# Order of the first conv buffers' state copies, and the place of the group norm among the z projections, in a hybrid pooling / SSD step

## The chip, the cores and the metric

The kernel runs on one core of one Trainium2 chip. The metric is device time in microseconds (us) of one execution; lower is better. A core has a matrix engine (PE, its weight loads shown as PEld), a vector engine (DVE), an activation engine (ACT), a general engine (POOL) and a queue engine (SP). In this kernel SP only issues loads of weights and activations; POOL issues most other transfers.

## The reference

One layer (DEPTH is 1) of a streaming encoder is computed for 384 rows of 2048 features: 256 rows of one new stream and 8 running streams of 16 rows. All data is float32.

```python
u = rmsnorm(x);  proj = u @ w_in          # columns: pool | z | x,B,C | dt | gates
A = pool_mixer(proj[pool])                # causal means of 2, 4, 8, 16 rows minus self, per-group map
xbc = silu(causal_conv(proj[xBC], state_conv))   # depthwise, width 4
y, h = ssd_scan(x, dt, A, B, C, h0)       # 64 heads of 64, state 128, 8 groups
y = y + d_skip * x
hg = y * silu(z)                          # gated norm: within each of the 8 groups of 512 columns
a_ssd = hg * rsqrt(mean(hg * hg) + EPS) * ssd_norm
m = sigmoid(gA) * (A @ w_pool_proj) + sigmoid(gB) * (a_ssd @ w_ssd_proj)
x = x + rmsnorm(m @ w_out)
x = x + rmsnorm(relu(rmsnorm(x) @ w_up) ** 2 @ w_down)
```

The last rows of the pooling and conv inputs and the SSD states are outputs too.

## The kernel before, in words

Every large product is made to float32 accuracy out of three products of a rounded format. A weight tile of 128x1024 is loaded by SP (`wfetch`), ACT copies its high part (`wh`, line 70) and DVE subtracts to get the low part (`wl`, line 71). PE then runs high by high (L101), high weight by low input (L102) and low weight by high input (L103). `wsplit` notes the last pair of such instructions in `cut`. There are three buffers each for the raw, the high and the low tile, and `take` keeps splits two half projections ahead of the one in use.

`proj` multiplies one 128-column block: two halves of 24 matmuls each. In the middle stage the eight SSD groups run one after the other. Group `g` has six projections with a convolution behind them (x, B, x, C, x, x) and four z projections (`zproj(0)` to `zproj(3)`). Among them PE does short products of the scan: those of the previous group's second pair of heads after the fifth conv projection, those of this group's first pair after the fourth z projection. The names that matter here:

- `conv_in`: DVE scales a projection into one of three conv buffers (L599). ACT then copies the three previous rows of each running stream out of the tile `cst_` ("cstate" in the profile) into the buffer (L606), passes the rows between blocks on (L607) and saves the new state (L608). `taps` does the convolution: ACT L616, three DVE L618, ACT L622 with the SiLU.
- `fside`: two DVE products on the decay tile E (L846). `dside`: a DVE product on the state `hs` (L852). `zproj` ends with a DVE scaling of its PSUM result into `zs` (L1039) and a SiLU on ACT (L1040). `final` forms `y` and `z*y` (L885, L896, L897), and squares are summed into `ssum` by ACT (L899, L902) and POOL (L903).
- `finish(prev)` calls `norm_bc` for the previous group: ACT rounds `ssum` (`nh_g`, L197), DVE makes the low part (`nl_g`, L198), PE sums over the partitions by two matmuls with a matrix of ones (`bc_g`: L201 reads `nh_g`, L202 reads `nl_g`), DVE scales the sum (L204), and ten more DVE instructions find the inverse root (L187 to L191). `store(prev)` (L913) scales the four `zs` tiles by it.

Each engine runs its own queue in order. The order of a queue is planned before the run: the planner goes by its own estimate of when each instruction's inputs are there, and among those that it holds to be ready it takes the one that stands first in the program. So instructions of an engine need not stand in the program's order. Two helpers add order: `behind(ins)` puts the instructions of a block that are on the engine of `ins` somewhere behind `ins`; `later()` does so for the last weight split on ACT and on DVE. The matmuls of a half projection are put behind the last matmul of the one before. The two matmuls of `norm_bc` are put behind the matmul that was last when `finish` was called.

Of the kernel before, what the change touches and what calls it, by code (L numbers as in the profile page):

```python
# [33 lines left out]
def build(ctx, tc, io):  # L34
# [21 lines left out]
    def behind(ins):  # L56
        return nullcontext() if ins is None else tc.issue_after(ins.ins)
# [19 lines left out]
    @contextmanager  # L77
    def later():
        with behind(cut[0]), behind(cut[1]):
            yield  # L80
# [10 lines left out]
    def even_odd(a):  # L91
        return a.rearrange("p (n a) -> p a n", a=2)

    def halves(a):
        return a.rearrange("p (a n) -> p a n", a=2)
# [40 lines left out]
    def proj(units, rhs, name, hook=None):  # L136
        o = bank[0](f"pj_{name}")[:, :T]
        for q, src in enumerate(units):
            half(o, q, take(src, f"{name}_{q}"), rhs)
            if hook:  # L140
                hook()
            tick()
        return o
# [50 lines left out]
    def norm_bc(pool, sumsq, n, name, after=None):  # L194
        h = pool.tile([P, T], F32R, tag="nr", name=f"nh_{name}", bufs=2)
        l = pool.tile([P, T], F32R, tag="nr", name=f"nl_{name}", bufs=2)
        s.activation(h, sumsq, AF.Copy)  # L197
        v.tensor_tensor(l, sumsq, h.bitcast(F32), ALU.subtract)  # L198
        o = sstile(f"bc_{name}")[:, :T]
        with behind(after):  # L200
            te.matmul(pairs(o), onesr, woven(h), start=True, stop=False)  # L201
            te.matmul(pairs(o), onesr, woven(l), start=False, stop=True)  # L202
        hm = sumsq
        v.tensor_scalar(halves(hm), even_odd(o), -0.5 / n, -0.5 * EPS, ALU.mult, ALU.add)  # L204
        a = pool.tile([P, T], F32, tag="nr", name=f"na_{name}", bufs=2)
        y = pool.tile([P, T], F32, tag="nr", name=f"ny_{name}", bufs=2)
        return newton(y, a, hm)
# [11 lines left out]
    def in_units(i):  # L219
        return [win[i - 5, 0], win[i - 5, 1]]  # L220
# [358 lines left out]
    with tc.tile_pool(name="phd", bufs=2, reuse_waits="tile") as pd, tc.tile_pool(  # L579
# [10 lines left out]
        ncv = [0]  # L590

        def conv_in(ui, c, hook=None):
            ps = proj(in_units(ui), xg, f"x{c}", hook)
            b = cbuf[ncv[0] % 3]
            ncv[0] += 1
            with later():
                for a in range(2):
                    c12 = slice(a * 12, a * 12 + 12)
                    v.tensor_tensor(  # L599
                        b[:, c12, 3:],  # L600
                        even_odd(ps)[:, a].rearrange("p (b t) -> p b t", b=12),
                        seg(rstd)[:, c12],
                        ALU.mult,
                    )
            with later() if 3 < ncv[0] <= 6 else behind(silu[0]):
                s.copy(b[:, 16:, :3], cst_[:, c, 1:])  # L606
            s.copy(b[:, 1:16, :3], b[:, 0:15, 16:])  # L607
            s.copy(cst_[:, c], b[:, 15:, 16:])  # L608
            return b

        silu = [None]
# [13 lines left out]
        def conv(ui, c, tag, nb, hook=None):  # L625
            return taps(conv_in(ui, c, hook), c, tag, nb)
# [50 lines left out]
        def pload(S):  # L677
            S.hs = pd.tile([P, NB, 2 * P], F32, tag="hs", name=f"hs{S.nm}")
            gp.dma_start(S.hs, io["ssm"][S.qd])
# [163 lines left out]
        def fside(S, h2):  # L843
            Eq = S.E[:, h2 * 2 : h2 * 2 + 2]
            with dve_later():
                v.tensor_tensor(Eq, Eq, S.D.cbm.unsqueeze(1).to_broadcast([P, 2, 512]), ALU.mult)  # L846

        def dside(S):
            hv = S.hs.rearrange("p b (h q) -> p b h q", h=4)
            dv = decb[:, S.h0 : S.h0 + 4, :].rearrange("p h b -> p b h").unsqueeze(3)  # L850
            with dve_later():
                v.tensor_tensor(hv, hv, dv.to_broadcast([P, NB, 4, 64]), ALU.mult)  # L852
# [52 lines left out]
        def finish(D):  # L905
            D.bc = norm_bc(pd, D.ssum, 512, f"g{D.g}", last[0])
# [26 lines left out]
        prev = None  # L933
        for g in range(G + 1):
# [34 lines left out]
            D.p = [pair(D, jp) for jp in range(2)]  # L969
            D.xs, D.zs = [], []  # L970
            b0 = conv_in(u0, g * 4)

            def first():
# [33 lines left out]
            if g:  # L1007
                fside(prev.p[1], 1)
            cside(D)
            b2 = conv_in(u0 + 4, g * 4 + 2)  # L1010
            S = D.p[0]
            S.py = mmtile(f"py{S.nm}")
# [22 lines left out]
            def zproj(j):  # L1035
                ps = proj(in_units(u0 + 6 + j), xg, f"z{g}_{j}")
                z = pd.tile([P, T], F32, tag="zs", name=f"zs{g}_{j}", bufs=8)
                with later():
                    v.tensor_tensor(halves(z), even_odd(ps), halves(rstd), ALU.mult)  # L1039
                    s.activation(z, z, AF.Silu)  # L1040
                D.zs.append(z)
# [7 lines left out]
                bside(D)  # L1049
            dside(S)  # L1050
            zproj(1)
            pload(D.p[1])
            fside(S, 0)
            fside(S, 1)
            zproj(2)
            if g:
                finish(prev)
            zproj(3)
            S1 = D.p[1]
            S1.py = mmtile(f"py{S1.nm}")  # L1060
# [10 lines left out]
            prev = D  # L1071
# [514 lines left out]
```

## Time and profile before

| | |
|---|---|
| time, three runs | 2636.21, 2636.32, 2637.59 us; median 2636.32 |
| profiled execution | 2635.75 us, of which the span of the instructions is 2633.9 |
| PE busy | 2622.0 us |
| PE weight load busy | 2523.3 us |
| DVE busy | 1572.8 us |
| ACT busy | 1160.2 us |
| POOL busy | 368.1 us |
| granted TensorE clock | 0.999 |

The SSD stage runs from about 419 us to 1200 us of the span. A row of the timeline gives the start, the duration, the engine, the line, the operation, the tiles (written<-read), shape, count, and in brackets how long the engine sat idle before it and what ended that. Rows of the same kind that follow each other are merged and counted (x2). The records of neighbours overlap a little. A row of the waits gives the waiting line and the one that released it, the total in us, the number of times, and the longest.

### The profile page before, as it was taken

To read this page: it belongs to the slowest core of one execution; us is meant where nothing else is said; L and a number is where in the kernel's file an instruction comes from. 1 tells how busy PE (TensorE), PEld (TensorE's weight loads), DVE (VectorE), ACT (ScalarE), POOL (GpSimd) and SP (SyncE) were. 2 spreads that over 40 slices of the span, in tenths; PEclk is the share of its full clock that TensorE was granted. 3 is DMA by queue.
4 is the path that set the end of the run, shared out by engine and by line. 5 is a ranking of instruction groups with operands and counts; after the bars stand their busy time and mean duration, and the time that the engine had idled before them with its cause. 6 is when DMAs were issued, how large, how long until landed. Compare 5 with 4: busy or idle time off the path is not lost.

```text
span 2633.9 us, 40787 instructions
## 1 busy us (share of the span) xinstructions
PE 2622.0 (100%) x16189; PEld 2523.3 (96%) x16189; DVE 1572.8 (60%) x2286; ACT 1160.2 (44%) x1789; POOL 368.1 (14%) x545
## 2 busy tenths in 40 slices
PE   9999999999999999999999999999999999999998
PEld 9999999999999999999999989999999999989897
DVE  6685335799999999867444336434444444444446
ACT  6443224657565756555333336433333333333233
POOL 0000002245344444421000000000000000000000
PEclk9999999999999999999999999999999999999999
DMA  7544446667676676657554544444444444444443
GB/s 276 149 134 156 147 148 218 205 207 239 223 239 211 234 230 236 225 190 261 169 160 160 192 149 133 142 137 134 135 135 136 135 136 136 136 136 136 135 135 130
DMA packets 134255, 456.33 MB, mean 173 GB/s; under 512 B 20544, under 2 KB 27520, under 8 KB 129072
## 3 DMA queue, kind: packets, MB, share of 16 engines
q1 hardware_dynamic: 103552, 361.44, 43.0%
q0 software_dynamic: 23456, 77.47, 8.4%
q10 hardware_dynamic: 7056, 14.81, 1.7%
q8 instruction: 127, 2.08, 0.3%
q14 instruction: 64, 0.52, 0.1%
HBM read 409.27 MB, written 44.37 MB: 172 GB/s over the span
## 4 chain that ended last, share of the span: by engine, by line
PE 96%; DMA 1%; DVE 1%; issue 1%; ACT 0%; POOL 0%; SPq 0%; DVEq 0%; POOLq 0%; ACTq 0%
PE pj_up L101 6%; PE pj_up L102 6%; PE pj_up L103 6%; PE wd L156 6%; PE wd L154 6%; PE wd L155 6%; PE pj_x L101 5%; PE pj_x L103 4%; PE pj_x L102 4%; PE pj_sp L103 3%; PE pj_sp L102 3%; PE pj_sp L101 3%; PE pj_z L103 3%; PE pj_z L102 3%; PE pj_z L101 3%; PE pj_gb L101 2%
## 5 line engine op out<-in xcount | busy, mean ns | idle before, releaser
L101 PE MATMUL pj_up<-x1h,wh_up 128*128 128x384 f32 (+1 forms) x1024 | 333.7, 326 | 0.0
L102 PE MATMUL pj_up<-x1l,wh_up 128*128 128x384 f32 (+1 forms) x1024 | 333.4, 326 | 0.0
L103 PE MATMUL pj_up<-x1h,wl_up 128*128 128x384 f32 (+1 forms) x1024 | 333.4, 326 | 0.0
L71 DVE TENSOR_TENSOR wl_wd<-w_wd,wh_wd 128x1024 fp32r<-128x1024 f32 x126 | 154.3, 1225 | 240.5 <-ACT wh_wd L70 240.5
L154 PE MATMUL wd<-wh_wd,hh 128*128 128x512 f32 x756 | 286.5, 379 | 0.0
L155 PE MATMUL wd<-wl_wd,hh 128*128 128x512 f32 x756 | 286.5, 379 | 0.0
L156 PE MATMUL wd<-wh_wd,hl 128*128 128x512 f32 x756 | 286.5, 379 | 0.0
L70 ACT ACTIVATE wh_wd<-w_wd 128x1024 fp32r<-128x1024 f32 x126 | 133.1, 1057 | 321.6 <-PE wd L156 261.2
L70 ACT ACTIVATE wh_up<-w_up 128x1024 fp32r<-128x1024 f32 x126 | 133.1, 1056 | 292.1 <-PE pj_up L102 231.7
L71 DVE TENSOR_TENSOR wl_up<-w_up,wh_up 128x1024 fp32r<-128x1024 f32 x126 | 154.3, 1225 | 178.2 <-ACT wh_up L70 178.0
L101 PE MATMUL pj_x<-xgh,wh_x 128*128 128x384 f32 x768 | 252.0, 328 | 0.0
L103 PE MATMUL pj_x<-xgh,wl_x 128*128 128x384 f32 x768 | 250.5, 326 | 0.7 <-DVE wl_x L71 0.7
L102 PE MATMUL pj_x<-xgl,wh_x 128*128 128x384 f32 x768 | 250.4, 326 | 0.0
L102 PEld LDWEIGHTS pj_up<-x1l,wh_up 128*128 128x128 f32 x1024 | 193.6, 189 | 0.2
L101 PEld LDWEIGHTS pj_up<-x1h,wh_up 128*128 128x128 f32 x1024 | 193.6, 189 | 0.2
L103 PEld LDWEIGHTS pj_up<-x1h,wl_up 128*128 128x128 f32 x1024 | 193.6, 189 | 0.0
L101 PE MATMUL pj_z<-xgh,wh_z 128*128 128x384 f32 x512 | 166.9, 326 | 0.0
L102 PE MATMUL pj_z<-xgl,wh_z 128*128 128x384 f32 x512 | 166.9, 326 | 0.0
L103 PE MATMUL pj_z<-xgh,wl_z 128*128 128x384 f32 x512 | 166.9, 326 | 0.0
L101 PE MATMUL pj_sp<-abh,wh_sp 128*128 128x384 f32 x512 | 166.9, 326 | 0.0
L102 PE MATMUL pj_sp<-abl,wh_sp 128*128 128x384 f32 x512 | 166.9, 326 | 0.0
L103 PE MATMUL pj_sp<-abh,wl_sp 128*128 128x384 f32 x512 | 166.9, 326 | 0.0
(351 smaller groups left out, 6371.5 us busy)
## 6 DMA issues: line engine op xcount, KB each, us to landing
w_up<-w_up SPq DMA_DIRECT2D x128, 512.0 KB, 3.4
w_wd<-w_down SPq DMA_DIRECT2D x128, 512.0 KB, 3.4
w_x<-w_in SPq DMA_DIRECT2D x96, 512.0 KB, 4.0
w_z<-w_in SPq DMA_DIRECT2D x64, 512.0 KB, 4.2
w_sp<-w_ssd SPq DMA_DIRECT2D x64, 512.0 KB, 3.5
w_ga<-w_ga SPq DMA_DIRECT2D x32, 512.0 KB, 3.6
w_pp<-w_pp SPq DMA_DIRECT2D x32, 512.0 KB, 3.5
hs<-ssm POOLq DMA_DIRECT2D x16, 1024.0 KB, 6.5
```

The lines of the kernel that those rows point to most:

```text
L70: cut[0] = s.activation(h, w, AF.Copy)
L71: cut[1] = v.tensor_tensor(l, w, h.bitcast(F32), ALU.subtract)
L101: te.matmul(out, wh, xh, start=first, stop=False, **how)
L102: te.matmul(out, wh, xl, start=False, stop=False, **how)
L103: return te.matmul(out, wl, xh, start=False, stop=last, **how)
L154: te.matmul(out, mh, vh, start=k == 0 and b != held, stop=False, skip_group_check=b == held)
L155: te.matmul(out, mh, vl, start=False, stop=False, skip_group_check=b == held)
L156: last[0] = te.matmul(out, ml, vh, start=False, stop=k == nk - 1, skip_group_check=b == held)
```

## The change

The copies of L606 for the first three conv buffers are put behind the last weight split, as those of buffers four to six already are. Before, the first had no such order, and the second and third were behind the last SiLU of a convolution (`silu[0]`). The call of `finish(prev)` in groups 1 to 7 moves from behind `zproj(2)` to behind `zproj(1)`, ahead of `pload` (a transfer that POOL issues) and of the two `fside` calls.

```diff
@@ -602,7 +602,7 @@
-            with later() if 3 < ncv[0] <= 6 else behind(silu[0]):
+            with later() if ncv[0] <= 6 else behind(silu[0]):
                 s.copy(b[:, 16:, :3], cst_[:, c, 1:])
             s.copy(b[:, 1:16, :3], b[:, 0:15, 16:])
             s.copy(cst_[:, c], b[:, 15:, 16:])
@@ -1049,12 +1049,12 @@
             dside(S)
             zproj(1)
+            if g:
+                finish(prev)
             pload(D.p[1])
             fside(S, 0)
             fside(S, 1)
             zproj(2)
-            if g:
-                finish(prev)
             zproj(3)
```

## The prediction

> **What bounds the kernel now.** I read the page first, then what PE waited for, then the timeline of DVE, PE, ACT and POOL through the z projections and round the start of the SSD stage. The page:
>
> ```profile
> span 2633.9 us, 40787 instructions
> PE 2622.0 (100%) x16189; PEld 2523.3 (96%) x16189; DVE 1572.8 (60%) x2286; ACT 1160.2 (44%) x1789; POOL 368.1 (14%) x545
> PE 96%; DMA 1%; DVE 1%; issue 1%; ACT 0%; POOL 0%; SPq 0%; DVEq 0%; POOLq 0%; ACTq 0%
> ```
>
> PE is busy for 2622.0 of 2633.9 us and makes 96% of the chain that ended last. Whatever the edits do to other engines counts only where PE waits. All that PE waited for (us in total, times, longest):
>
> ```profile
> PE warm_o L242 <- DVE warm L238: 1.2, 1, 1.2
> PE su L861 <- DVE xs L885: 0.9, 1, 0.9
> PE pj_x L103 <- DVE wl_x L71: 0.7, 1, 0.7
> PE pj_p L103 <- DVE wl_e L304: 0.3, 1, 0.3
> PE pj_p L318 <- DVE xgl L280: 0.2, 1, 0.2
> ```
>
> That is 3.3 us, of which the first, fourth and fifth lie far ahead of anything edited. So the change can win at most 0.9 + 0.7 = 1.6 us, or 0.06%. It can lose much more: every new wait of PE is added to the span as it stands, and there are seven groups in which `finish` moves. About 0.2% (5.3 us) is what a measurement of this kernel can tell from no change.
>
> **The norm moved, its instructions.** `finish` has one ACT, two PE and twelve DVE instructions (L198, L204 and ten of the root) and no transfer; their number and sizes stay. DVE in the z phase of group 1, where z1 and z2 stand for the second and third z projection:
>
> ```profile
> 570.50 2.35 DVE L71 TENSOR_TENSOR wl_z<-w_z,wh_z 128x1024 fp32r<-128x1024 f32 x2
> 572.77 2.36 DVE L846 TENSOR_TENSOR E<-E,cbm 128x1024 f32<-128x1024 f32 x2
> 575.04 0.55 DVE L1039 TENSOR_TENSOR zs<-pj_z,rstd 128x384 f32<-128x384 f32 x1
> 575.50 1.22 DVE L71 TENSOR_TENSOR wl_z<-w_z,wh_z 128x1024 fp32r<-128x1024 f32 x1
> 576.64 0.55 DVE L198 TENSOR_TENSOR nl_g<-ssum,nh_g 128x384 fp32r<-128x384 f32 x1
> 577.13 1.23 DVE L71 TENSOR_TENSOR wl_z<-w_z,wh_z 128x1024 fp32r<-128x1024 f32 x1
> 579.82 0.56 DVE L1039 TENSOR_TENSOR zs<-pj_z,rstd 128x384 f32<-128x384 f32 x1 [1.47 <-PE pj_z L103]
> 580.29 0.55 DVE L204 TENSOR_SCALAR ssum<-bc_g 128x384 f32<-128x384 f32 x1
> 580.80 1.22 DVE L71 TENSOR_TENSOR wl_x<-w_x,wh_x 128x1024 fp32r<-128x1024 f32 x1
> 588.08 0.56 DVE L191 SCALAR_TENSOR_TENSOR ny_g<-na_g,ny_g 128x384 f32<-128x384 f32 x1
> ```
>
> The row at 570.50 holds the low parts of both halves of z2, that at 575.04 takes the result of z1. The PE rows are z1's last matmul, the first two of z2, and the norm's first product in groups 1 and 7:
>
> ```profile
> 571.66 0.33 PE L103 MATMUL pj_z<-xgh,wl_z 128*128 128x384 f32 x1
> 571.82 0.33 PE L101 MATMUL pj_z<-xgh,wh_z 128*128 128x384 f32 x1
> 571.98 0.33 PE L102 MATMUL pj_z<-xgl,wh_z 128*128 128x384 f32 x1
> 579.62 0.33 PE L201 MATMUL bc_g<-nh_g,onesr 128*128 128x384 f32 x1
> 1105.59 0.33 PE L201 MATMUL bc_g<-nh_g,onesr 128*128 128x384 f32 x1
> ```
>
> Before, the norm's products came at 579.62, right behind z2, and `nl_g` had been ready since 577.19. That left 2.6 us of slack up to L202 at 579.78. Between group 1 and group 7 lie 1105.59 - 579.62 = 525.97 us, so a group takes 87.66.
>
> After the change the products belong right behind z1: L201 at 571.82, L202 at 571.98. Their other inputs are there:
>
> ```profile
> 554.88 4.00 POOL L903 TENSOR_TENSOR ssum<-ssum,ysq 128x384 f32<-128x384 f32 x1 [0.41 <-ACT ysq L902]
> 567.18 0.51 ACT L197 ACTIVATE nh_g<-ssum 128x384 fp32r<-128x384 f32 x1
> ```
>
> The sum ends at 558.88 and `nh_g` at 567.69, both well ahead. What is not there is `nl_g`. DVE is behind at this point: the low parts of z2 end at 572.85, 0.9 us after z1 has ended (571.99), and z1's result is fetched 3 us late.
>
> **Where `nl_g` will stand.** Ahead of the new `finish` in the program stand the splits of z2 and the scaling of z1; behind it the two E products. `nl_g` was ready from 567.69 on but never ran ahead of the z2 splits, so the planner saw no gap for it there, and the move does not lift it over instructions that still precede it. It does lift it over E. So I put `nl_g` where the first E stands, at 572.77, ending at 573.32.
>
> **Where the two products will stand.** The planner put two E products ahead of the scaling of z1, although that stands earlier in the program. So when it chose the second E, one E product (1.2 us) after the z2 splits, it held z1 to be unfinished still. In its account DVE finishes the z2 splits over 1.2 us before z1 ends; in the trace it does 0.9 us after. The planner is thus out by some 2 us, and an `nl_g` of 0.55 us ends, by its account, some 0.6 us or more before z1 does. The norm's products are then ready when z1 ends, and stand ahead of z2 in the program. They are placed between z1 and z2, and z2's 48 matmuls queue behind L202.
>
> **The sum of the new waits.** In each group L202 has its turn at 571.98 + 87.66 (g - 1), and `nl_g` ends 0.55 us after the start of the first E. The hand-over to PE is taken from the wait of `su` quoted below: L885 ends at 1118.46, PE starts at 1118.51, 0.05 us. The starts of E in groups 2 to 7:
>
> ```profile
> 660.46 2.35 DVE L846 TENSOR_TENSOR E<-E,cbm 128x1024 f32<-128x1024 f32 x2
> 748.30 2.35 DVE L846 TENSOR_TENSOR E<-E,cbm 128x1024 f32<-128x1024 f32 x2
> 836.05 2.35 DVE L846 TENSOR_TENSOR E<-E,cbm 128x1024 f32<-128x1024 f32 x2
> 924.53 2.35 DVE L846 TENSOR_TENSOR E<-E,cbm 128x1024 f32<-128x1024 f32 x2
> 1011.10 2.35 DVE L846 TENSOR_TENSOR E<-E,cbm 128x1024 f32<-128x1024 f32 x2
> 1100.03 2.35 DVE L846 TENSOR_TENSOR E<-E,cbm 128x1024 f32<-128x1024 f32 x2
> ```
>
> E's start + 0.60 less the turn of L202 gives, for groups 1 to 7: 1.39, 1.42, 1.60, 1.69, 2.51, 1.42, 2.69, together 12.7 us. Group 5 is larger because its second split waited for ACT's high part:
>
> ```profile
> 923.39 1.23 DVE L71 TENSOR_TENSOR wl_z<-w_z,wh_z 128x1024 fp32r<-128x1024 f32 x1 [1.03 <-ACT wh_z L70]
> ```
>
> Bounds: if the planner lets three of z2's matmuls (0.16 us apart) in ahead of the products, each wait is 0.5 us shorter, 9.2 us in all. If it takes E first and the products only when `nl_g` is ready by its account, each wait approaches its error of 2 us or a little over, up to 17.5 us in all at 2.5 each. I take 12.7, the one that the rows give.
>
> **What else moves.** L204 and the ten of the root (580.29 to 588.64, with other splits between) come some 6 us earlier, where DVE has other work and 1.47 us idle. PE can lose there only if z3's low parts come late. They were done at 576.72 and 578.36; the first is wanted from 579.94 (z3 begins one matmul, 0.16 us, behind L202 at 579.78), the second 24 matmuls later, at 583.8, and both later still by PE's new wait. The root is a chain in which each step needs the one before, and in the rows above a split that stands later in the program (580.80) was let in behind its first step, L204. So z3's splits will be let in too. I cost this at nothing; the cover is 3.2 us on the first half. A root put wholly ahead of it takes some 6 us of DVE (eleven steps of 0.56), and would cost PE about 2 us a group. `pload` is a POOL issue that `finish` has no instruction in front of. The E products slip by 0.5 us or more and are wanted by the scan's products only behind z3.
>
> **What goes.** In group 7 alone PE waited in the state update:
>
> ```profile
> 1117.85 0.61 DVE L885 SCALAR_TENSOR_TENSOR xs<-xs,vec,Y 128x384 f32<-128x384 f32 x1
> 1118.51 0.71 PE L861 MATMUL su<-xd,Bd 32*128 32x256 f32 x13 [0.94 <-DVE xs L885]
> ```
>
> The root ran ahead of L885 on DVE; in group 1 it ends at 588.64, which in group 7 corresponds to 588.64 + 525.97 = 1114.6, and L885 came at 1117.85. With the root moved to z2's window, eleven DVE instructions that stand ahead of L885 are out of its way by then, and the 0.94 goes. Next late there would be what released the other six groups, in which PE did not wait.
>
> **The copies.** The other wait of 0.7 us is that of the fifth half projection on its low part:
>
> ```profile
> 425.25 0.54 POOL L583 DMA_DIRECT2D cstate<-state_conv  x1 [4.58 <-DMA ma_scr<-sg]
> 422.78 1.06 ACT L70 ACTIVATE wh_x<-w_x 128x1024 fp32r<-128x1024 f32 x1 [2.84 <-PE pj_x L102]
> 433.32 0.22 ACT L606 COPY cbuf<-cstate 128x24 f32<-128x24 f32 x1 [9.48 <-DMA cstate<-state_conv]
> 433.44 1.06 ACT L70 ACTIVATE wh_x<-w_x 128x1024 fp32r<-128x1024 f32 x1
> 438.82 0.62 ACT L622 ACTIVATE xs<-cacc,vec 128x384 f32<-128x384 f32 x1 [1.31 <-DVE cacc L618]
> 439.34 0.20 ACT L606 COPY cbuf<-cstate 128x24 f32<-128x24 f32 x1
> ```
>
> ACT waits for the state's transfer with the next split (433.44) queued behind the copy. When the first `conv_in` reaches its copy, the last split is the fourth of the stage, 422.78; the copy stands behind that already. The new order adds nothing, and the wait stays. The second and third copies are freed from the SiLU before them and can use ACT's idle time (1.31 us ahead of 438.82), 0.2 us each. No PE wait follows there. I cost this edit at 0, between -0.7 (the copy goes behind the fifth split after all) and +0.5 (a freed copy pushes a split, two copies and a gap).
>
> **Sum.** 12.7 - 0.94 + 0 = 11.8 us. The profiled execution, 2635.75, would be 2647.5; it is 0.57 below the median of the runs, so the median becomes 2648.1.
>
> **Rivals.**
> *No wait behind z1.* The planner finds `nl_g` a place ahead of the z2 splits (say at 570.50), or puts the products deep into z2, 1.4 to 2.7 us behind its start. Then PE waits for nothing new, the 0.94 goes, and the time is 2636.3 - 0.9 = 2635.4, with the copies at best 2634.7. It decides once `nl_g` ends before its product's turn, 1.8 us (12.7 / 7) earlier than I place it in the mean group. For it: `nh_g` is ready at 567.69, 2.8 us ahead of the z2 splits. Against it: `nl_g` was just as free to go there before and did not.
> *Long waits.* E, E and the scaling of z1 run ahead of `nl_g`, and the products still stand right behind z1: 2.8 us more in each group (2.36 + 0.47), 12.7 + 7 x 2.8 = 32.3 us, 2636.3 + 32.3 - 0.9 = 2667.7. Against it: the planner does not put E ahead of what stands earlier and is ready.
> [...]
> *The change does nothing to the order that matters*: `nl_g` and the products land where they were, 2636.3.
>
> **How the numbers follow.** The forecast gets 0.63, no wait 0.26, long waits 0.05, nothing 0.06. The forecast's own range is from 2636.3 + 9.2 - 0.9 - 0.7 = 2643.9, to 2636.3 + 17.5 - 0.9 + 0.5 = 2653.4. The range to hold 8 in 10 needs the no-wait rival as well: 2635.0 to 2653.0. Slower by over 0.2% means above 2641.6: the forecast but for 0.02 of it, and the long waits, 0.66. Within 0.2%: no wait, nothing, and that 0.02, less 0.01, is 0.33. Faster by over 0.2% would need more than PE now waits for in all, 0.01.
>
> **What would show it.** Right: among PE's waits `bc_g` L202 for DVE `nl_g`, seven times, 1.4 to 2.7 us; L201 right behind z1 in each group; `nl_g` between the z2 splits and the first E; no wait of `su`; the wait of `pj_x` still about 0.7. Wrong: `bc_g` with no wait, or L201 in the midst of z2, or `nl_g` ahead of the z2 splits; or a new wait of `pj_z` L103 on a split, which would mean that the root stands ahead of it.

## The result, and the profile after

The changed kernel took 2648.84 us in the median of six runs (2646.74 to 2652.73), the kernel before 2636.32 in six (2635.30 to 2637.59): a ratio of 1.005, 95% interval 1.0037 to 1.0063. That is 12.5 us slower, against the forecast 2648.1. In the profiled execution (2647.98 us) the span grew by 12.3 us, from 2633.9 to 2646.2. The head of the page, and all that PE waited for:

```profile
span 2646.2 us, 40773 instructions
PE 2624.9 (99%) x16189; PEld 2525.1 (95%) x16189; DVE 1572.8 (59%) x2286; ACT 1160.6 (44%) x1789; POOL 368.2 (14%) x545
...
PE bc_g L202 <- DVE nl_g L198: 11.0, 7, 2.6
PE warm_o L242 <- DVE warm L238: 1.2, 1, 1.2
PE su L861 <- DVE xs L885: 0.2, 1, 0.2
PE pj_p L318 <- ACT xgh L278: 0.2, 1, 0.2
PE pj_p L103 <- DVE wl_e L304: 0.2, 1, 0.2
```

One new line carries the change: the norm's second product waits for the low part of its sum, seven times. The 0.7 us of `pj_x` are gone and the 0.9 of `su` have become 0.2. DVE's busy time is the same to a tenth; nothing was added, things came in another order. DVE in the z phase of group 1, to be held against the rows from 570.50 to 577.13 of before:

```profile
568.84 2.35 DVE L71 TENSOR_TENSOR wl_z<-w_z,wh_z 128x1024 fp32r<-128x1024 f32 x2
571.11 0.55 DVE L198 TENSOR_TENSOR nl_g<-ssum,nh_g 128x384 fp32r<-128x384 f32 x1
571.58 2.35 DVE L846 TENSOR_TENSOR E<-E,cbm 128x1024 f32<-128x1024 f32 x2
573.85 0.55 DVE L1039 TENSOR_TENSOR zs<-pj_z,rstd 128x384 f32<-128x384 f32 x1
574.32 0.54 DVE L204 TENSOR_SCALAR ssum<-bc_g 128x384 f32<-128x384 f32 x1
574.78 1.21 DVE L71 TENSOR_TENSOR wl_z<-w_z,wh_z 128x1024 fp32r<-128x1024 f32 x1
575.91 0.35 DVE L187 TENSOR_SCALAR ny_g<-ssum 128x384 int32<-128x384 int32 x1
```

`nl_g` stands between the splits of the third z projection (z2) and the first E, where it was placed in the prediction. The split of the last one (574.78) was let in between two steps of the root. On PE the norm's products are now directly behind the second projection (z1). In group 1, then in group 7, with what follows it:

```profile
570.14 0.33 PE L201 MATMUL bc_g<-nh_g,onesr 128*128 128x384 f32 x1
571.71 0.43 PE L202 MATMUL bc_g<-nl_g,onesr 128*128 128x384 f32 x1 [1.25 <-DVE nl_g L198]
...
1106.80 0.33 PE L201 MATMUL bc_g<-nh_g,onesr 128*128 128x384 f32 x1
1109.77 0.43 PE L202 MATMUL bc_g<-nl_g,onesr 128*128 128x384 f32 x1 [2.64 <-DVE nl_g L198]
1110.04 0.33 PE L101 MATMUL pj_z<-xgh,wh_z 128*128 128x384 f32 x1
1110.20 0.33 PE L102 MATMUL pj_z<-xgl,wh_z 128*128 128x384 f32 x1
1110.36 0.49 PE L103 MATMUL pj_z<-xgh,wl_z 128*128 128x384 f32 x1
1110.64 0.53 PE L101 MATMUL pj_z<-xgh,wh_z 128*128 128x384 f32 x1
...
1113.52 0.47 PE L101 MATMUL pj_z<-xgh,wh_z 128*128 128x384 f32 x1
1113.83 0.33 PE L102 MATMUL pj_z<-xgl,wh_z 128*128 128x384 f32 x1
```

Two costs stand here that the listed 11.0 us do not hold. First, matmuls that follow each other start 0.16 us apart, but L202 comes 0.16 us later behind L201 than the listed wait alone makes it (571.71 - 570.14 = 1.57 against 1.25 + 0.16), and the next matmul comes 0.27 us behind L202 (1110.04 - 1109.77), 0.1 more than usual: about 0.27 us for each wait. Second, behind group 7's wait ten matmuls or so start 0.32 us apart. From 1110.36 to 1113.83 there are eleven steps, which take 3.47 us where 1.8 is usual: 1.7 us more. The table by stretches shows the granted clock there (the first number behind POOL's; the last two are the DMA share and GB/s), after and then before; from 1110.36 to 1113.83 alone it is 0.51 after:

```profile
1104.00:1113.00 9.00, 6.36 (x32) 6.06 (x31) 7.73 (x9) 2.63 (x3) 5.41 (x9) 0.85 0.98 345
```

```profile
1104.00:1113.00 9.00, 9.00 (x57) 9.00 (x56) 6.87 (x12) 3.65 (x4) 2.95 (x5) 1.00 0.77 266
```

The account: 11.0 listed, 7 x 0.27 = 1.9 around the waits, 1.7 of half clock, less 0.7 of `su`, less 0.9 of `pj_x` (0.67 and 0.27 around it). That is 13.0. From the stage's first conv matmul to the last L101 matmul of the gate projections behind it PE took 828.8 us before and 841.6 after, 12.8 more. The span grew by 0.5 less than that, because in the profile after the stage began 0.5 us earlier (418.31 against 418.85).

### The profile page after: what moved, and what is told of

The parts are those of the page before. It is cut to its first block, busy times and chain, and to the rows that moved or that the text cites. A ratio compares the mean times of both kernels' runs of the same rounds, so it can differ in the third digit from the quotient of the medians.

```text
span 2646.2 us, 40773 instructions
## 1 busy us (share of the span) xinstructions
PE 2624.9 (99%) x16189; PEld 2525.1 (95%) x16189; DVE 1572.8 (59%) x2286; ACT 1160.6 (44%) x1789; POOL 368.2 (14%) x545
## 4 chain that ended last, share of the span: by engine, by line
PE 88%; DVE 7%; issue 2%; DMA 1%; ACT 1%; POOL 0%; SPq 0%; DVEq 0%; ACTq 0%; POOLq 0%
PE pj_up L103 6%; PE pj_up L101 6%; PE pj_up L102 6%; PE wd L156 6%; PE wd L155 6%; PE wd L154 6%; PE pj_sp L102 3%; PE pj_sp L103 3%; PE pj_sp L101 3%; PE pj_x L101 3%; PE pj_x L102 3%; PE pj_x L103 3%; PE pj_z L101 2%; PE pj_z L102 2%; PE pj_z L103 2%; PE pj_gb L101 2%
## 5 line engine op out<-in xcount | busy, mean ns | idle before, releaser
L101 PE MATMUL pj_up<-x1h,wh_up 128*128 128x384 f32 (+1 forms) x1024 | 333.7, 326 | 0.0
L101 PE MATMUL pj_x<-xgh,wh_x 128*128 128x384 f32 x768 | 251.9, 328 | 0.0
L101 PEld LDWEIGHTS pj_up<-x1h,wh_up 128*128 128x128 f32 x1024 | 193.6, 189 | 0.2
L101 PE MATMUL pj_z<-xgh,wh_z 128*128 128x384 f32 x512 | 167.7, 327 | 0.0
L101 PE MATMUL pj_sp<-abh,wh_sp 128*128 128x384 f32 x512 | 166.9, 326 | 0.0
```

The source lines that it names most:

```text
L101: te.matmul(out, wh, xh, start=first, stop=False, **how)
```

## The experiments

Each time stands beside runs of the kernel before on the same chip. PE's waits are those of the profiled execution. The diffs are against the changed kernel where nothing else is said.

**Which of the two edits.** The norm's call alone moved:

```diff
-            with later() if ncv[0] <= 6 else behind(silu[0]):
+            with later() if 3 < ncv[0] <= 6 else behind(silu[0]):
```

> Only the norm is moved behind the second z projection; the copies keep their old order. Theory (PE waits in L202 for the low part nl_g, seven times): the whole loss is here, 2646 to 2651 us, bc_g L202 waits for nl_g seven times, 10 to 13 us in all, no wait of su over 0.3 us. Rival (the copies carry a share of the loss): clearly under 2646, with fewer or shorter waits of L202.

Measured: 2646.55 us (2645.30 to 2649.86), ratio 1.0044 (1.0030 to 1.0057). PE's first wait is the same line:

```profile
PE bc_g L202 <- DVE nl_g L198: 10.9, 7, 2.6
```

The copies alone:

```diff
             zproj(1)
-            if g:
-                finish(prev)
...
             zproj(2)
+            if g:
+                finish(prev)
             zproj(3)
```

> Only the copies of the first three conv buffers are put behind the weight splits; the norm stays behind the third z projection. Theory: nothing on the path, 2635.5 to 2637.0 us, the wait of pj_x for its low part stays between 0 and 1 us as the state's transfer happens to land, su still waits about 0.9. Rival (the freed copies push weight splits): 2638 us or more, with a new wait of pj_x. Rival (the copies are what took the 0.7 us wait away in the changed kernel): 2635.6 or less in every round, pj_x wait gone.

Measured: 2635.56 us (2634.22 to 2638.42), ratio 1.0000 (0.9991 to 1.0009). So all of the loss is the norm's, and the copies are worth nothing that can be measured. The wait of `pj_x` is not in this profile; why it comes and goes is told with the copies below.

**Is it nl_g's place on DVE, or the products' place on PE?** The call stays behind z1, but the low part is computed behind the first z projection, so that only the products and the root behind them are at the new place:

```diff
-    def norm_bc(pool, sumsq, n, name, after=None):
+    def norm_split(pool, sumsq, name):          # L196 to L198: nh and nl
...
+        return h, l
+
+    def norm_bc(pool, sumsq, n, name, after=None, hl=None):
+        h, l = hl or norm_split(pool, sumsq, name)
...
             zproj(0)
+            if g:
+                prev.nhl = norm_split(pd, prev.ssum, f"g{prev.g}")
```

> As the changed kernel, but the ACT and DVE halves of the norm's input (nh_g, nl_g) are called behind the first z projection; the two PE products stay behind the second. Theory: nl_g then ends before its product's turn, the seven waits go, 2634.8 to 2637.0 us, and at most 0.1 us a group is lost on z2's split, which comes 0.5 us later with 0.4 us of slack. Rival (the products between z1 and z2 cost PE by themselves, or the root on DVE does): 2645 us or more, with no wait of L202 for nl_g.

Measured: 2633.85 us (2632.82 to 2635.54), ratio 0.9992 (0.9983 to 1.0000). Its DVE and PE rows (its lines are numbered four higher from here on), and all of PE's waits:

```profile
562.77 0.55 DVE L198 TENSOR_TENSOR nl_g<-ssum,nh_g 128x384 fp32r<-128x384 f32 x1
...
570.35 0.33 PE L205 MATMUL bc_g<-nh_g,onesr 128*128 128x384 f32 x1
570.51 0.33 PE L206 MATMUL bc_g<-nl_g,onesr 128*128 128x384 f32 x1
...
PE warm_o L246 <- DVE warm L242: 1.2, 1, 1.2
PE pj_p L103 <- DVE wl_e L308: 0.2, 1, 0.2
PE pj_p L322 <- ACT xgh L282: 0.2, 1, 0.2
```

The products and the root stand as early as in the changed kernel and cost nothing; with `nl_g` eight microseconds earlier the second follows the first by 0.16 us. The loss is the low part alone.

**Does a later call help?** `finish` is called in the middle of z2, by a hook between its halves:

```diff
             zproj(1)
-            if g:
-                finish(prev)
...
+            halves_done = []
+
+            def mid_norm():
+                halves_done.append(1)
+                if g and len(halves_done) == 1:
+                    finish(prev)
+
-            zproj(2)
+            zproj(2, mid_norm)
```

> finish is called in the middle of the third z projection, half a projection (3.9 us) later than in the changed kernel, behind the fside products. Theory: nl_g falls behind E, E, the scaling of z1 and z3's first split on DVE, as in the kernel before (start 576.64 in group 1), L202 has its turn at 575.88, so PE waits again, 1.4 to 2.7 us a group: 2644 to 2650 us. Rival (3.9 us more distance is more than the longest wait of 2.6 us, so the waits go): 2635 to 2637 us.

Measured: 2648.06 us (2647.29 to 2650.67), ratio 1.0049 (1.0035 to 1.0063); seven waits, 10.7 us in all. In group 1:

```profile
576.12 0.33 PE L201 MATMUL bc_g<-nh_g,onesr 128*128 128x384 f32 x1
577.67 0.43 PE L202 MATMUL bc_g<-nl_g,onesr 128*128 128x384 f32 x1 [1.22 <-DVE nl_g L198]
```

Six microseconds later on PE, and the wait is the same: `nl_g` moved back behind both E products, the scaling of z1 and a split. A distance in the program is no distance in time while DVE's queue moves along with it.

**Does an earlier call help?** `finish` is called behind the first z projection (z0):

```diff
             zproj(0)
+            if g:
+                finish(prev)
...
             zproj(1)
-            if g:
-                finish(prev)
```

> The finish of the group before is called behind the first z projection instead of the second; the copies as in the changed kernel. Theory (a wait of L202 is the place of nl_g on DVE less the place of the products on PE, and both move with the call): nl_g comes right behind the evacuations that precede the first z projection, ahead of its second weight split, so the products find it after a shorter way: about 0.7 us of wait in each of the seven groups and 0.27 us of drain and refill with each, 2635.5 + 7 x 0.95 = about 2642 us (2637 to 2645). Rival (the earlier the call, the further DVE is behind PE, since the E products and the evacuation of y stand ahead of it): waits of 1.4 us and more in each group, 2648 us or more. Rival (the place of the products itself costs, whatever DVE does): 2648 us with no waits of L202 to show for it.

Measured: 2639.66 us (2638.48 to 2640.47), ratio 1.0016 (1.0006 to 1.0025).

```profile
PE bc_g L202 <- DVE nl_g L198: 3.7, 7, 0.6
```

Seven waits of 0.5 us each, where the theory had 0.7: at that place DVE is behind PE by less. Longer waits, or the time without the waits, as the rivals had it, are not there.

**Taking DVE work from in front of nl_g instead.** The changed kernel with `dside` (2.3 us on the state `hs`) behind the E products:

```diff
-            dside(S)
             zproj(1)
...
             fside(S, 0)
             fside(S, 1)
+            dside(S)
```

> The changed kernel with the D-side work of the next step (dside) moved from ahead of the second z projection to behind the two F-sides; the call of the norm's finish stays behind the second z projection. That takes about 2.3 us of DVE work from in front of nl_g. Theory (the wait is DVE's queue in front of nl_g): no wait of L202 above 0.3 us is left, 2636 us (2634.5 to 2638.5). Rival (the products or the root cost PE time of themselves when they stand between the second and the third z projection): still 2648 us. Rival (what is moved comes late at its new place and TensorE waits for it there): a new wait on the y side's operands, 2642 us or more.

Measured: 2636.02 us (2634.69 to 2638.12), ratio 1.0002 (0.9993 to 1.0011). In group 1 (DVE, then PE), and PE's waits:

```profile
568.09 0.55 DVE L198 TENSOR_TENSOR nl_g<-ssum,nh_g 128x384 fp32r<-128x384 f32 x1
...
570.46 0.33 PE L201 MATMUL bc_g<-nh_g,onesr 128*128 128x384 f32 x1
570.62 0.33 PE L202 MATMUL bc_g<-nl_g,onesr 128*128 128x384 f32 x1
...
PE pj_z L103 <- DVE wl_z L71: 3.3, 3, 1.7
PE warm_o L242 <- DVE warm L238: 1.2, 1, 1.2
```

The wait of L202 is gone with the products where the change put them. The third rival was half right: there is a new wait, but not on the y side's operands. In groups 3, 5 and 7 PE waits 0.44, 1.09 and 1.73 us for the first low part of the last z projection (z3), because the moved `dside` (L852) now stands ahead of that split on DVE. In group 7 (DVE, then PE):

```profile
1105.10 2.28 DVE L852 TENSOR_TENSOR hs<-hs,decb 128x2048 f32<-128x2048 f32 x1
...
1107.58 1.21 DVE L71 TENSOR_TENSOR wl_z<-w_z,wh_z 128x1024 fp32r<-128x1024 f32 x1
...
1108.84 0.43 PE L103 MATMUL pj_z<-xgh,wl_z 128*128 128x384 f32 x1 [1.73 <-DVE wl_z L71]
```

Groups 5 and 7 had the longest waits of L202 too: in the changed kernel DVE's second split of z2 itself waits there for ACT's high part, 0.67 and 1.27 us. `su` and `pj_x` do not wait in this run, which pays for part of the new wait.

**What sets the length of a wait.** The low part written five times:

```diff
-        v.tensor_tensor(l, sumsq, h.bitcast(F32), ALU.subtract)
+        for _ in range(5): v.tensor_tensor(l, sumsq, h.bitcast(F32), ALU.subtract)
```

> The changed kernel with the low part nl_g written five times over (the same values), so about 4 x 0.5 us of DVE work more in front of the second product in each group, and other DVE work let in between. Theory (the products are placed by the planned end of nl_g, and the wait is what the plan is off by): the products move back on TensorE with the longer chain and the wait stays near 1.3 to 2.6 us a group: 2646 to 2656 us. Rival (the products stand fixed behind the second z projection): each wait grows by all that DVE does between the five, 4 to 6 us a group, 2635.5 + 7 x 7 = about 2685 us.

Measured: 2671.15 us (2669.23 and 2673.08), ratio 1.0136 (1.0115 to 1.0156), between the two expectations. The same with the third z projection made to follow the second product:

```diff
-            te.matmul(pairs(o), onesr, woven(l), start=False, stop=True)
+            last[0] = te.matmul(pairs(o), onesr, woven(l), start=False, stop=True)
```

> As the run before, but the third z projection is made to follow the second product, so that TensorE has nothing else to do while the five writes of nl_g go by. Theory: a wait of about 5 to 7 us in each of the seven groups, 2635.5 + 7 x 6 = 2678 us (2665 to 2695), at a granted clock as in the kernel before. [...]

Measured: 2704.97 us (2704.90 and 2705.03), ratio 1.0264 (1.0244 to 1.0285). Group 1 of the first, then group 1 of the second:

```profile
571.34 0.33 PE L201 MATMUL bc_g<-nh_g,onesr 128*128 128x384 f32 x1
...
575.56 0.33 PE L102 MATMUL pj_z<-xgl,wh_z 128*128 128x384 f32 x1
578.69 0.43 PE L202 MATMUL bc_g<-nl_g,onesr 128*128 128x384 f32 x1 [2.80 <-DVE nl_g L198]
```

```profile
572.69 0.33 PE L201 MATMUL bc_g<-nh_g,onesr 128*128 128x384 f32 x1
580.04 0.69 PE L202 MATMUL bc_g<-nl_g,onesr 128*128 128x384 f32 x1 [7.02 <-DVE nl_g L198]
580.52 0.53 PE L101 MATMUL pj_z<-xgh,wh_z 128*128 128x384 f32 x1
```

In the first the planner moved the second product 26 matmuls into z2 (571.50 to 575.56, 0.1625 us each), as the theory had it, and still put it 2.80 us too early, against 1.25 in the changed kernel: with more DVE work let in ahead the plan was further out. I had expected the wait to stay. In the second the wait is the whole chain, 7.02 us; the 4.2 us between are the 26 matmuls. All of PE's waits of L202, first and second:

```profile
PE bc_g L202 <- DVE nl_g L198: 21.8, 7, 4.1
```

```profile
PE bc_g L202 <- DVE nl_g L198: 52.3, 7, 9.6
```

The rest of their loss is the clock. Behind 13 of the 14 waits matmuls start 0.32 us apart for 8 to 18 of them; counted over the stage, what they take beyond 0.16 is 10.3 us in the first and 13.7 in the second above what slow steps make in the kernel before. The granted clock of the span is 0.994 and 0.988, against 0.999 before. Account of the second: 52.3, with 7 x 0.48 = 3.4 around the waits, and 13.7, less 1.2 of `su` (0.94 and 0.27), make 68.2; the span grew by 2703.1 - 2633.9 = 69.2. The expected range, at the clock of the kernel before, ended at 2695.

Not every wait has this behind it, and its length alone does not tell which has. Matmuls start 0.32 us apart behind waits of 1.97 and 2.30 us (the middle-of-z2 kernel's groups 5 and 7), of 2.64 (the changed kernel's group 7), of 2.76 to 4.12 (groups 2 to 7 of the first of the two kernels) and of 6.97 to 9.61 (all seven groups of the second). They stay 0.16 us apart behind the 2.01 us of the changed kernel's group 5 and behind the 2.80 us of the first kernel's group 1, though behind a wait of the same length in its group 2 they do not. Group 1 of that kernel, then its group 2:

```profile
578.69 0.43 PE L202 MATMUL bc_g<-nl_g,onesr 128*128 128x384 f32 x1 [2.80 <-DVE nl_g L198]
578.96 0.33 PE L103 MATMUL pj_z<-xgh,wl_z 128*128 128x384 f32 x1
579.12 0.33 PE L101 MATMUL pj_z<-xgh,wh_z 128*128 128x384 f32 x1
579.28 0.33 PE L102 MATMUL pj_z<-xgl,wh_z 128*128 128x384 f32 x1
...
669.42 0.69 PE L202 MATMUL bc_g<-nl_g,onesr 128*128 128x384 f32 x1 [2.80 <-DVE nl_g L198]
669.90 0.53 PE L103 MATMUL pj_z<-xgh,wl_z 128*128 128x384 f32 x1
670.22 0.53 PE L101 MATMUL pj_z<-xgh,wh_z 128*128 128x384 f32 x1
670.54 0.53 PE L102 MATMUL pj_z<-xgl,wh_z 128*128 128x384 f32 x1
```

What else it hangs on is left open.

**The copies and the wait of pj_x.** The kernel before with the first buffer's three copies issued from the hook in the second projection (`edges` holds the copies of L606 to L608):

```diff
+            if defer:
+                return b
             with later() if 3 < ncv[0] <= 6 else behind(silu[0]):
-                s.copy(b[:, 16:, :3], cst_[:, c, 1:])
+                edges(b, c)
...
-            b0 = conv_in(u0, g * 4)
+            b0 = conv_in(u0, g * 4, defer=not g)
...
                     with later():
+                        edges(b0, 0)
                         first()
```

> The kernel before, with the first conv buffer's three copies taken out of ScalarE's order and issued from the second conv projection, so that the copy that waits for the state's transfer no longer stands ahead of the splits of that projection. Theory (the wait of pj_x for wl_x, 0.67 us in the kernel before and absent from the changed kernel, is the landing of the state's transfer and not the copies' place behind one or two splits): no wait of pj_x for wl_x in the first projections, whenever the transfer lands; 0.7 to 0.9 us less, 2634.5 to 2636, which a ratio of 0.9997 with an interval of some 0.001 can't tell from 1. Rival (the splits are late of themselves, by their weights): the wait stays at 0.6 us or so.

Measured: 2635.51 us (2634.09 to 2637.37), ratio 0.9996 (0.9987 to 1.0005); no wait of `pj_x`. What decides that wait shows across the profiles. The first row is the norm alone (copies in the old order), the next two the middle-of-z2 kernel (copies in the new order):

```profile
430.09 0.21 ACT L606 COPY cbuf<-cstate 128x24 f32<-128x24 f32 x1 [6.72 <-DMA cstate<-state_conv]
```

```profile
433.73 0.22 ACT L606 COPY cbuf<-cstate 128x24 f32<-128x24 f32 x1 [9.23 <-DMA cstate<-state_conv]
...
436.21 0.43 PE L103 MATMUL pj_x<-xgh,wl_x 128*128 128x384 f32 x1 [0.62 <-DVE wl_x L71]
```

Old order, early landing: no wait. New order, late landing: the wait is there. In the changed kernel's profile the copy came at 431.33, and there is none. Ten profiles have this copy at its old place in ACT's order. In the four where it came at 432.85 or later PE waits 0.48 to 0.67 us, in the six where it came at 431.85 or earlier it does not wait, and both groups have kernels with the old and with the new order. So it is the landing of the state's transfer, which differs by some 4 us from run to run, and not the edit. That the deferral makes the wait go whenever the transfer lands is likely by its construction but not shown: in both profiles with the deferral the transfer landed early, 4.8 and 6.1 us after its issue (at 424.79 and 424.28), so by 430.4 at the latest.

**Both gains together.** The early low part (its diff above) and the deferred copies (the diff just shown, in place of the change's edit to L605):

> The low part nl_g computed early (behind the first z projection), its products behind the second, and the first conv buffer's copies deferred as in the run beside it. Theory: neither bc_g nor su nor pj_x waits; 2633.0 to 2635.0 (two to three us below the kernel before: 0.94 + 0.27 of su's wait, 0.67 + 0.27 of pj_x's). Rival (the early low part's gain of 0.0008 was the spread of the runs): 2635.5 to 2637.

Measured: 2634.06 us (2632.64 to 2634.91), ratio 0.9991 (0.9982 to 1.0000); `bc_g`, `su` and `pj_x` all wait for nothing. It is 2.3 us below its kernel before, as the early low part alone was 2.6 below: the two agree, and each interval just reaches 1. A gain of about 0.09% is likely, but not beyond doubt; the deferral adds none that can be seen.

## Why the prediction was right

- **PE bounds.** Right: PE's waits and PE's clock account for the change in time.
- **The place of nl_g, and of the products.** Right in all seven groups: `nl_g` where the first E had been, L201 directly behind z1. The other candidate places are ruled out by the rows shown. The reason given, that the planner's own account runs some 2 us ahead of the chip, stays argued: no run shows the planner's times.
- **The size of the waits.** The rule "E's start + 0.60 less the turn of L202" gave 1.39 for group 1; L202 came 1.41 us late (571.71 against 570.14 + 0.16). Over the seven groups the delays (listed wait and 0.16) make 1.41, 1.50, 1.41, 1.43, 2.17, 1.44 and 2.80, together 12.2 against 12.7.
- **Left out.** The 0.1 us by which the matmul behind each wait is late, 0.7 in all, and the half clock behind group 7's wait of 2.64 us, 1.7. Why the runs of the changed kernel spread over 6 us stays open. More of these spells in some runs, at 1.7 us each, could do it, but only one of the six executions has a trace here, and the mean granted clock of the others (0.998 or 0.999) can't count spells: this one reads 0.999 with one spell in the stage, the profile of the kernel before 0.999 with none.
- **su.** Mostly right: group 7's 0.94 went, but 0.21 appeared in group 2, which was not forecast. It is in neither the norm-alone nor the early-low-part profile. That the root's place makes the 0.94 is borne out: the two profiles with `finish` at its old place, copies alone and the deferred copies, keep such a wait (1.2 and 1.0 us), and none with an earlier call has one over 0.21.
- **The root at no cost.** Right: a split was let in between its steps, and PE waits for no split of the last z projection.
- **The copies.** The edit at 0 is right (1.0000, 0.9991 to 1.0009). "The wait of `pj_x` still about 0.7" failed in the profile after: it was read as a fixed cost of the order when it is one of the transfer's landing, which the row at 433.32 named as releaser.

So the total came out right with two errors that partly cancel: about 1.9 too little for what a wait brings with it (0.7 + 1.7, less 0.5 that the delays were under the forecast), and 0.9 too much for the `pj_x` wait that was held to stay; 11.8 - 0.5 + 0.7 + 1.7 + 0.2 - 0.9 = 13.0.

## What to carry to other kernels

Before a short product is moved up in a saturated matrix engine's queue, look where its last operand stands in the other engine's queue at that moment: if that engine is behind, the operand's own step must be moved up first, by its own call, or work must be taken from in front of it. Count for each new wait more than the listed idle time (0.27 us more in the changed kernel), and look for slower matmuls behind it (1.7 us lost behind group 7's wait there, nothing behind the other six). A wait that ends on a transfer belongs to that run until several profiles show it.

## What the hardware showed unexpectedly

- PE's matmuls went to half rate (0.32 us apart for 0.16) behind a wait of 1.97 us, and kept full rate behind one of 2.01 and one of 2.80. Behind the 14 waits with the low part written five times, 13 spells lasted 8 to 18 matmuls, 0.16 us lost on each.
- A wait of L202 cost about 0.27 us beyond its listed length where the next matmul came at full clock (the changed kernel), about 0.48 where it came at half clock (z2 held: 0.16 ahead of L202, 0.32 behind it).
- The same transfer of the conv state (648 KB) ended its reader's wait between 430.09 and 434.20 us of the span, with its issue on POOL between 423.79 and 425.66.
